# Key loads of an attention kernel: one DMA with a repeated source, or two DMAs of 64 rows

## The chip, the cores and the metric

The kernel runs on one core of one Trainium2 chip. The metric is the device time of one execution in microseconds, as the median of several runs. All durations in the rows below come from one execution that the hardware profiler recorded.

## What is computed

A two-layer encoder trunk for one prompt of 1024 positions and for 8 short groups of 16 positions with caches (1152 rows in all, width 1024). Layer 0 has sliding-window attention with 16 query heads over 4 key heads, a window of whole 64-row chunks, a sink for each head and a relative-position bias. Layer 1 has banded attention with 16 heads, each with its own keys and values, which are projected once from the output of layer 0. Each layer ends with an output projection, a normalisation and a gated feed-forward block with a short causal convolution. Cut to the attention:

```python
s = jnp.einsum('bqkgd,bskd->bkgqs', qg, k) * ATTN_SCALE + bias
s = jnp.where(valid, s, NEG_INF)          # own chunk and the 2 (layer 0) or 8 (layer 1) before it
p = softmax(s)                            # layer 0: with one more term, the sink
o = jnp.einsum('bkgqs,bskd->bqkgd', p, v)
```

## The kernel before, in words

Every float32 operand of a large product is held as two parts, a rounded high part and the rest as a low part, and a product is made of several matmuls of such parts.

The kernel projects queries, keys and values by matmul (mmT, L266, and mmX, L278). The keys of a layer are projected in `kproj` (L287): ScalarE (ACT) copies the high part out of PSUM (L297), VectorE (DVE) computes the low part (L298), and SyncE (SP) stores both to the DRAM tensor `kH` (L299), one row for each of the head's 64 dimensions and one column for each of 1024 positions. Values go the same way to `vH` in `vproj` (L326 to L328).

`attention` (L338) runs over 8 pairs `c` of heads and two heads `a` in each, and over 4 groups of 256 queries for each head, so 64 work items a layer. For one head it holds in SBUF the high keys `khi[a]`, the low keys `klo[a]` (128 partitions by 1024 columns) and the values `vst[a]`. The 64 key rows stand twice in a key tile, in partitions 0 to 63 and 64 to 127, because the query tile has the high part of the query in one half of the partitions and the low part in the other: one matmul with 128 rows (L504 with `khi`, L507 with `klo`) then makes two of the products. `kload` (L429) fills these tiles; `klo[1]` lies in the tile `wl`, the other three key tiles in `x1att`, and so the rows name them. A load of the next pair's head is issued from `finish` (L692), when the last scores and values of the present head with the same `a` are in the program: layer 1 does this for each head (L698), layer 0, where a key head serves four query heads, once for each `a` (L700).

After the scores come the softmax (DVE L470, ACT L474), the transposes of the probabilities (PE L530, split by ACT L535 and DVE L536), the products with the values (PE L549) and the store of the result from the Pool queue (L564). Between the heads, the 16 `items` of the small groups are worked off: their cached keys and values are loaded by SP (L597, L598, L603, L605), the value product is PE L650. Also between them, the query weights of the next pair (L164) and, towards the end of layer 1, the first weights of the output projection (`ws<-in_wo`, L164) are loaded; ACT rounds them (L149) and Pool or DVE takes the difference (L160).

All loads and stores but the bias loads, the attention output and the normalised rows are issued by SP, in one order, on one hardware queue (q1). Each engine works through its own instructions in order. That order comes from a scheduling pass that works with modelled durations when the kernel is built (L1340), not from the program's text alone.

Of the kernel before, what the change touches and what calls it, by code (L numbers as in the profile page):

```python
# [10 lines left out]
F32 = mybir.dt.float32  # L11
# [76 lines left out]
class Trunk:  # L88
# [249 lines left out]
    def attention(self, l, wk):  # L338
        nc, I = self.nc, self.I
# [76 lines left out]
        for p in range(2):  # L416
            t = sb.next()[:, 0:KS]
# [11 lines left out]
        def kload(c, a):  # L429
            row = c * 128 + 64 * a  # L430
            kh, kl = kH[0, row : row + 64, :], kH[1, row : row + 64, :]
            for t, k in ((khi[a], kh), (klo[a], kl)):
                nc.sync.dma_start(t.bitcast(F32), bass.AP(k.tensor, k.offset, [[0, 2], [1024, 64], [1, 1024]]))
            nc.sync.dma_start(
                vst[a].bitcast(F32), vH[:, 2 * c + a, :].rearrange("(k p) d -> p k d", p=128)
            )
# [255 lines left out]
        def finish(i):  # L692
            x = work[i]
            values(x)
            if x.g == 3:
                c, a = x.head.c, x.head.a
                if l == 1 and c < 7:
                    kload(c + 1, a)  # L698
                elif l == 0 and c == 3:
                    kload(1, a)  # L700
            if i == 6 * 8 - 1:
                sums(0)

        for a in range(2):
            kload(0, a)
# [638 lines left out]
```

## Time and profile before

| what | us |
|---|---|
| median of 3 runs | 3324.27 |
| lowest and highest run | 3322.79, 3326.6 |
| the profiled execution | 3324.77 |
| its span, from the first to the last instruction | 3322.8 |

The profile page gives, for each engine, the busy time and a strip of 40 slices of the span; each digit is the busy share of a slice of 83 us in tenths. PEclk is the granted clock of TensorE in tenths of full speed. The DMA strip is the mean busy share of 16 DMA engines. Attention of layer 0 is at about 85 to 440 us, the key and value projections of layer 1 at about 1580 to 1794 us, its attention at about 1794 to 2291 us. The feed-forward blocks fill most of the rest.

### The profile page before, as it was taken

The page shows a single profiled execution, that of the slowest core. Times are in us where ns is not written, and L with a number is a line of the kernel's source. Part 1 is how long each engine was busy: PE and PEld are TensorE (multiplying, and loading weights), DVE is VectorE, ACT ScalarE, POOL GpSimd, SP SyncE. Part 2 cuts the span into 40 slices and gives each one's busy share as a digit, 9 for nine tenths or more (in the row PEclk, how much of TensorE's full clock was granted, in tenths as well). Part 3 has the DMA queues.
Part 4 walks back from the last instruction along what each step waited for, and adds up shares of the span by engine and source line. Part 5 has one row for each costly group of instructions (what it writes and reads, how often), then busy time and mean ns, then how long its engine had stood idle before and what let it go on. Part 6 is the DMA issues. An engine that isn't in the chain of part 4 may idle for free. (4 is left out here: it accounts for less than half of the span.)

```text
span 3322.8 us, 42663 instructions
## 1 busy us (share of the span) xinstructions
PE 2927.7 (88%) x16524; PEld 2598.2 (78%) x16524; DVE 1553.0 (47%) x3162; ACT 1130.4 (34%) x2400; POOL 920.5 (28%) x745
## 2 busy tenths in 40 slices
PE   7697967899999999998898687656789999999996
PEld 5685755788888888887898676545679999999995
DVE  4253656524444444477014454335583444444457
ACT  3263622432222222226226454333244222222224
POOL 3021212423222222354531111110253222222253
PEclk8898988999999999999999897878899999999998
DMA  7343485622222222225664334347731111111121
GB/s 285 122 132 131 140 182 128 203 102 80 86 82 85 87 80 92 67 65 202 220 222 136 104 113 133 122 124 196 154 125 45 45 39 45 44 43 38 39 75 73
DMA packets 216282, 372.78 MB, mean 112 GB/s; under 512 B 34168, under 2 KB 138424, under 8 KB 215696
## 3 DMA queue, kind: packets, MB, share of 16 engines
q1 hardware_dynamic: 205808, 336.49, 32.6%
q0 software_dynamic: 10272, 33.56, 2.9%
q8 instruction: 130, 2.13, 0.3%
q14 instruction: 72, 0.59, 0.1%
HBM read 294.65 MB, written 84.79 MB: 114 GB/s over the span
## 5 line engine op out<-in xcount | busy, mean ns | idle before, releaser
L266 PE MATMUL PS<-H,wh 128*128 128x384 f32 (+1 forms) x5472 | 1060.7, 341 | 0.3 <-DVE H L160 0.3
L266 PEld LDWEIGHTS PS<-H,wh 128*128 128x128 f32 x5472 | 976.8, 190 | 17.1 <-issue 7.3
L266 PE MATMUL PS<-H,wl 128*128 128x384 f32 (+1 forms) x2736 | 575.5, 348 | 55.4 <-DVE X L327 22.7
L160 POOL TENSOR_TENSOR wl<-ws,wh 128x1024 fp32r<-128x1024 f32 x167 | 405.8, 2436 | 744.0 <-ACT wh L149 732.3
L981 DVE SCALAR_TENSOR_TENSOR F<-PS,F 128x256 f32<-128x256 f32 (+2 forms) x704 | 352.5, 512 | 491.7 <-ACT F L978 480.4
L266 PEld LDWEIGHTS PS<-H,wl 128*128 128x128 f32 x2736 | 495.0, 193 | 97.3 <-issue 43.8
L1052 PE MATMUL PS<-wh,X 128*128 128x512 f32 x1584 | 470.7, 396 | 18.4 <-DVE X L160 9.0
L978 ACT ACTIVATE F<-PS,F 128x384 f32<-128x384 f32 x264 | 177.2, 672 | 727.7 <-PE PS L266 724.7
L1052 PEld LDWEIGHTS PS<-wh,X 128*128 128x128 f32 x1584 | 294.9, 189 | 82.1 <-DVE X L160 11.0
L1043 DVE TENSOR_TENSOR acc<-acc,PS 128x512 f32<-128x512 f32 x324 | 221.4, 686 | 274.8 <-PE PS L1052 273.9
L1027 POOL TENSOR_TENSOR F<-F 128x384 f32<-128x384 f32 x132 | 138.9, 1053 | 649.3 <-ACT F L1025 643.8
L1052 PE MATMUL PS<-wl,X 128*128 128x512 f32 x792 | 247.1, 393 | 0.0
L149 ACT CAST wh<-ws 128x1024 fp32r<-128x1024 f32 x176 | 181.7, 1043 | 151.7 <-PE PS L1052 75.0
L278 PE MATMUL PS<-wh,H 128*128 128x256 f32 (+1 forms) x1008 | 199.4, 327 | 33.4 <-DVE H L160 24.9
L160 DVE TENSOR_TENSOR X<-F,X 128x384 fp32r<-128x384 f32 x132 | 151.6, 1149 | 99.6 <-ACT X L149 97.2
L278 PEld LDWEIGHTS PS<-wh,H 128*128 128x128 f32 x1008 | 154.3, 198 | 49.0 <-DVE H L160 26.1
L1052 PEld LDWEIGHTS PS<-wl,X 128*128 128x128 f32 x792 | 149.4, 189 | 33.6
L564 POOL DMA_DIRECT2D oT<-F x96 | 52.3, 545 | 441.3 <-ACT F L561 324.3
L530 PE MATMUL PS<-C,F 128*128 128x128 f32 x720 | 127.4, 294 | 38.1 <-DVE X L536 21.8
L470 DVE CUSTOM_DVE_ANT_0 F<-PS,F,C 128x256 f32<-128x256 f32 (+3 forms) x208 | 96.8, 480 | 93.9 <-PE PS L507 61.6
L470 DVE CUSTOM_DVE_ANT_0 F<-PS,F 128x320 f32<-128x320 f32 (+5 forms) x144 | 67.5, 480 | 142.8 <-issue 64.3
L530 PEld LDWEIGHTS PS<-C,F 128*128 128x128 f32 x720 | 90.5, 150 | 54.5 <-DVE X L536 24.0
(200 smaller groups left out, 3304.8 us busy)
## 6 DMA issues: line engine op xcount, KB each, us to landing
ws<-in_wup_dram SPq DMA_DIRECT2D x88, 512.0 KB
F<-in_adaw_dram SPq DMA_DIRECT2D x74, 512.0 KB
ws<-in_wdn_dram SPq DMA_DIRECT2D x44, 512.0 KB
ws<-in_adaw_dram SPq DMA_DIRECT2D x32, 512.0 KB
X<-oT SPq DMA_DIRECT2D x64, 256.0 KB
x1att<-kH SPq DMA_DIRECT2D x30, 512.0 KB
F<-xd SPq DMA_DIRECT2D x27, 512.0 KB
vH<-X SPq DMA_DIRECT2D x40, 256.0 KB
```

What stands on the lines that cost most here:

```text
L149: nc.scalar.copy(out, in_)
L160: self.eng(el).tensor_sub(lo, src, hi.bitcast(F32))
L266: self.nc.tensor.matmul(out[:, 0:n], w[a][:, k * 128 : k * 128 + 128], H[:, p, k, s0 : s0 + n], start=i == 0, stop=i == 23)
L278: self.nc.tensor.matmul(out[:, 0:n], H[:, p, j * kn + k, t0 : t0 + 128], w[a][:, k * n : k * n + n], start=i == 0, stop=i == 23,)
L470: nc.vector.tensor_tensor_reduce(out=p[:, c0 : c0 + w], in0=ps, in1=b, scale=1.0, scalar=init, op0=ALU.add, op1=ALU.min, accum_out=nm)
L530: nc.tensor.transpose(t[:, m * 128 : m * 128 + 128], p[:, (kt - k0) * 128 : (kt - k0) * 128 + 128], self.ident)
L564: nc.gpsimd.dma_start(self.oT[c, a, :, g0 : g0 + og * 256], x.head.o)
L978: nc.scalar.activation(y, ps[:, off : off + 384], AF.Identity, bias=w(3), scale=w(2))
L981: nc.vector.scalar_tensor_tensor(o, u, w(i), o, op0=ALU.mult, op1=ALU.add)
L1027: nc.gpsimd.tensor_mul(a, y, ya[bi])
L1043: nc.vector.tensor_add(row[:, n], row[:, n], ps)
L1052: nc.tensor.matmul(ps, ac[m][p][:, cs], w[m][q][:, n], start=i == 0, stop=i == 5)
```

## The change

`kload` issued one DMA for each key tile, whose source names the 64 rows twice through a leading dimension of 2 with step 0. It now issues two DMAs for each key tile, each from the plain 64 rows to one half of the partitions. The value load stays as it is. `kload` is called 20 times (4 times in layer 0, 16 times in layer 1), so 40 key DMAs of 512 KB become 80 of 256 KB.

```diff
             for t, k in ((khi[a], kh), (klo[a], kl)):
-                nc.sync.dma_start(t.bitcast(F32), bass.AP(k.tensor, k.offset, [[0, 2], [1024, 64], [1, 1024]]))
+                for b in range(2):
+                    nc.sync.dma_start(t[64 * b : 64 * b + 64, :].bitcast(F32), k)
```

## Rows read from the trace of the kernel before

**Rows 1.** The profile page: busy time by engine, strips of 40 slices
```profile
PE 2927.7 (88%) x16524; PEld 2598.2 (78%) x16524; DVE 1553.0 (47%) x3162; ACT 1130.4 (34%) x2400; POOL 920.5 (28%) x745
PE   7697967899999999998898687656789999999996
```

**Rows 2.** Waits of PE, 1780 to 2300 us: waiter, releaser, total us, times, longest
```profile
PE PS L507 <- DMA x1att<-kH: 51.2, 6, 13.1
PE PS L650 <- DMA F<-in_cvB_dram: 32.8, 4, 21.6
PE PS L530 <- DVE X L536: 21.8, 1, 21.8
PE PS L530 <- DVE wh L536: 14.5, 1, 14.5
PE PS L504 <- DVE x1att L457: 11.5, 1, 11.5
PE PS L507 <- DMA wl<-kH: 10.2, 1, 10.2
PE PS L504 <- DMA x1att<-kH: 3.1, 2, 2.2
```

**Rows 3.** Timeline of PE elsewhere: start, length, instruction, [idle before it, releaser]
```profile
123.32 2.90 PE L266 MATMUL PS<-H,wl 128*128 128x384 f32 x8 [22.65 <-DVE X L327]
264.42 0.48 PE L507 MATMUL PS<-x1att 128*128 128x128 f32 x1 [8.75 <-DMA x1att<-kH]
292.18 0.48 PE L507 MATMUL PS<-wl,x1att 128*128 128x128 f32 x1 [9.06 <-DMA wl<-kH]
1632.06 2.93 PE L266 MATMUL PS<-H,wl 128*128 128x384 f32 x8 [11.89 <-ACT F L305]
```

**Rows 4.** Windows: us; busy of PE, PEld, DVE, ACT, POOL; PEclk; DMA share; GB/s
```profile
88.00:93.00 5.00, 5.00 (x44) 5.00 (x43) 0.00 (x0) 0.00 (x0) 0.00 (x0) 1.00 0.13 52
...
1603.00:1608.00 5.00, 5.00 (x31) 5.00 (x30) 0.56 (x1) 0.48 (x1) 0.24 (x1) 1.00 0.13 52
...
2033.00:2038.00 5.00, 0.00 (x0) 0.00 (x0) 0.00 (x0) 0.00 (x0) 0.00 (x0) 0.50 0.13 52
```

**Rows 5.** Timeline of SP: start, length of the issue, line, transfer
```profile
1593.31 10.54 SPq L433 DMA_DIRECT2D x1att<-kH  x3
1603.89 9.93 SPq L299 DMA_DIRECT2D kH<-X  x1
...
1830.20 10.47 SPq L434 DMA_DIRECT2D x1att<-vH  x1
1840.71 10.62 SPq L433 DMA_DIRECT2D wl<-kH  x1
```

**Rows 6.** The chain that ended last, 1817 to 1850 us: start, us, what
```profile
1817.50 27.36 DMA x1att<-kH
1844.86 0.04 issue
```

**Rows 7.** Waits of ACT and DVE, 1780 to 2300 us
```profile
ACT x1att L149 <- DMA ws<-in_wo_dram: 39.5, 3, 21.0
DVE F L884 <- DMA F<-hmD: 11.9, 1, 11.9
```

**Rows 8.** Waits of ACT, whole span
```profile
ACT X L297 <- DMA kH<-X: 48.9, 9, 26.4
ACT X L326 <- DMA vH<-X: 37.8, 4, 23.1
```

**Rows 9.** Windows: after a stall, the whole attention of layer 1, and its ends
```profile
1845.00:1850.00 5.00, 5.00 (x16) 4.81 (x17) 2.02 (x5) 0.60 (x2) 0.00 (x0) 0.50 0.15 55
1872.00:1877.00 5.00, 5.00 (x35) 4.96 (x34) 1.93 (x7) 1.53 (x5) 0.84 (x3) 1.00 0.20 81
...
1795.00:1797.00 2.00, 2.00 (x8) 2.00 (x8) 1.94 (x4) 1.45 (x2) 0.00 (x0) 0.50 0.72 220
2289.00:2291.00 2.00, 0.99 (x7) 0.79 (x8) 2.00 (x3) 0.86 (x3) 0.55 (x1) 1.00 0.22 71
1795.00:2291.00 496.00, 351.98 (x2537) 312.14 (x2537) 225.51 (x707) 225.16 (x569) 69.30 (x115) 0.82 0.39 120
```

**Rows 10.** A window of the output projection, where SP issues 64-partition loads (L921)
```profile
2303.00:2306.00 3.00, 3.00 (x15) 2.43 (x14) 0.87 (x2) 0.22 (x1) 0.00 (x0) 1.00 1.22 229
```

**Rows 11.** Key load line: issue ns shortest, median, longest; first and last start
```profile
L433 SPq DMA_DIRECT2D x1att<-kH x30: 484/525/10615, 82.9 to 2213.1; - x30
```

**Rows 12.** The chain near the end: one weight load of 512 KB
```profile
3208.23 3.17 DMA ws<-in_wdn_dram
```

**Rows 13.** Timeline of SP, end of layer 1's attention: cached values of two items
```profile
2247.76 0.37 SPq L603 DMA_DIRECT2D F<-in_cvB_dram  x1
...
2258.07 0.37 SPq L603 DMA_DIRECT2D F<-in_cvB_dram  x1
```

## The prediction

> **What bounds the kernel now.** I first read the page: PE is busy for 88% of the span, and its strip shows where it is not [rows 1]. The weak stretch that touches this change is the run of sixes and fives around slices 22 to 27, the attention of layer 1. Next I asked who PE waits for in that stretch [rows 2]. The longest sum is a wait of the score matmuls for key tiles: 51.2 us on `x1att<-kH`, 10.2 us on `wl<-kH` and 3.1 us more at L504, 64.5 us in all. The window of the whole stretch [rows 9] has PE busy for 352 of 496 us, so 144 us idle, and nearly half of that names a key load directly. Two more such waits stand in layer 0, 8.75 and 9.06 us [rows 3].
>
> Then I asked why a key load is late. The chain shows one that took 27.36 us from issue to landing [rows 6], where a weight load of the same 512 KB took 3.17 us [rows 12]. The windows tell why: in three places where key loads alone were under way, the DMA share is 0.13 and the rate 52 GB/s [rows 4]. A share of 0.13 of 16 engines is two engines (2/16 = 0.125), and 524,288 bytes at 52 GB/s take 10.1 us. SP's timeline has the same number a third time: once some loads are queued, SP sits 10.47 and 10.62 us in a single issue, and it does so too for a value load and for a key store that merely come after key loads [rows 5]. So a key load runs on two of 16 engines for 10.1 us, and whatever SP has queued behind it, which needs those two engines as well, waits for it.
>
> That explains waits that do not name a key load. ACT waits for a weight of the output projection, 39.5 us in three waits [rows 7]; ACT works in order, so its PSUM copies of probabilities stop, and PE's transposes wait 21.8 and 14.5 us for an engine that itself has nothing to do [rows 2]. PE waits 32.8 us for cached values, `in_cvB` [rows 2]. DVE waits 11.9 us for `hmD` [rows 7] and hands that on to PE as 11.5 us at the first scores of layer 1 [rows 2]. ACT waits up to 23.1 us for a value store and 26.4 us for a key store to free a buffer [rows 8], which PE sees as 22.65 us at 123 us and as 11.89 us at 1632 us [rows 3].
>
> **The change, part by part.** *The transfer.* Two DMAs of 64 rows take the place of one whose source begins with a dimension of 2. The trace of before has no key load in the new form. Its nearest row is the window in which SP issues loads into 64 partitions [rows 10]: the DMA share is over 1 there (packet times overlap), so such loads use all 16 engines, not two. Bounds for a 512 KB tile: at the long end it stays at 10.1 us plus one more issue; at the short end it takes 1.3 us (two engines moved 52 GB/s, so 16 would move 416). I take the weight load's 3.17 us to landing [rows 12], since it is the nearest in size and in runs of 4 KB.
>
> The trace says 0.13 and 52 GB/s for the present form [rows 4]. [...]
>
> *SP's issue time.* 40 more issues, median 0.525 us each [rows 11], are 21 us of SP. They lie beside SP's blocked time: single issues of over 10 us [rows 5] go away, so I count nothing. If SP were the bound they would cost these 21 us.
>
> *The direct waits.* A load was issued at 1817.50 and PE began to wait 13.1 us before 1844.9, at 1831.8, so PE has 14.3 us of other work after the issue [rows 2, 6]. The new load of both tiles needs four issues, 2.1 us, and some 3.2 us to landing, 5.3 us together. It fits, so these waits go: 64.5 + 8.75 + 9.06 = 82.3 us.
>
> *The waits behind it.* 32.8 (cached values), 21.8 + 14.5 (weights through ACT), 11.5 (`hmD`), 22.65 (value stores) and 11.89 (key stores) sum to 115.1 us. Each has a transfer of its own that remains, so I give back about 2 us for each of some nine waits, 18 us.
>
> *The clock.* [...] The product of busy time and missing clock over all 248 windows of 2 us from 1795 to 2291 us (the first and the last are shown) sums to 37.6 us [rows 9]. Less stall means less of this; I keep back a quarter, 9 us.
>
> *What is late next.* Between stalls PE is busy 5.00 of 5.00 us at full clock [rows 9]: it is the bound as soon as the keys are there. DVE and ACT each have 225 us of work in the 496 [rows 9], which is 72% of the 314 us (352 - 37.6) that PE needs at full clock. Their queues drain today while PE stalls, and that rest goes away. The items keep one tile for cached values, and the next load can start only when the last one was used: even late in the stretch two such loads stand 10.3 us apart [rows 13], while two work items of PE will take about 2 x 314/64 = 9.8 us. The cost of both lies between 0 and some 40 us; I take 20 us.
>
> *Sum.* 82.3 + 115.1 + 37.6 = 235 us of losses that hang on the two busy engines; 18 + 9 + 20 = 47 us given back; gain 188 us. The profiled execution took 3324.77 us (3322.8 us of span and 2 us around it), half a microsecond over the median of the runs, so no correction is needed: 3324.8 - 188 = 3137 us.
>
> **The rivals.** (A) Forecast: 16 engines, the queue clears, PE becomes the bound. 3137 us; its own range is 3090 (nothing given back) to 3180 (twice the 47 us and no more).
>
> (B) The key waits go, but half of the rest comes back under other names, because ACT and DVE at 72% or the chain of the items hold PE. 82.3 + 0.5 x (115.1 + 37.6) = 159 us, less 47, is 112: 3213 us. For it: the order of each engine's work comes from modelled durations and will not fit the new transfers; every wait of PE passes through an in-order ACT. Against: in the stretches between stalls PE has no gap at all.
>
> (C) Everything comes back, and smaller waits that I left out as well: 3080 to 3090 us.
>
> (D) The change doesn't do what it says: each half still runs on two engines. Then the two halves need 5.05 us each, 10.1 us as before, and time stays at 3325 us. If in addition the 40 more issues lie on the path, 21 us come on top: 3346 us, slower. It decides at one point, the number of engines that a 64-row load gets. Against it stands the share over 1 for 64-partition loads [rows 10].
>
> **How the numbers follow.** I give (A) 0.70, (B) 0.19, (C) 0.06, and (D) 0.05, of which 0.02 without the cost of the issues and 0.03 with it. The likeliest gives 3137 us. The range for 8 in 10 has to take in (A), part of (B) and the edge of (C): 3080, the low end of (C), to 3215, just past the value of (B). About 0.2% of the time, 7 us, is what a measurement of this kernel can tell from no change: faster by more than that 0.95, within it 0.02, slower 0.03.
>
> **What would show it right or wrong.** In the profile after: the key load line should have 80 issues, none near 10 us, and no window of busy transfers at a share of 0.13 and 52 GB/s in the attention. SP should hardly be blocked in an issue. The waits of PE on `x1att<-kH` and `wl<-kH` should be under some 10 us in sum, the two long waits at L530 and ACT's wait for `in_wo` should be small, and the wait of 22.65 us at 123 us should be a few us. The granted clock of layer 1's attention should be above 0.95 and its length about 340 to 360 us. It would be wrong if key loads still move at 52 GB/s (then D), or if they move fast and PE's waits turn up at L504, L530 or L650 behind DVE, ACT or `in_cvB` (then B).

## The result, and the profile after

| | us |
|---|---|
| before, median (4 runs) | 3325.43 |
| after, median (4 runs) | 3090.66 |
| after, lowest and highest | 3085.17, 3098.18 |
| span of the profiled execution after | 3088.3 |
| ratio after to before, with its 95% interval | 0.9295 [0.9274, 0.9317] |

The change takes 234.8 us off, 7.1% of the time. Lines of the kernel below the key loads have a number one higher than before (L504 is now L505, and so on); in the runs k2 to k8 and p2 to p16 further down it is two higher.

The page after, busy times and the strip of PE (40 slices of 77 us), answers to [rows 1]:

```profile
PE 2884.1 (93%) x16524; PEld 2566.4 (83%) x16524; DVE 1545.2 (50%) x3162; ACT 1130.1 (37%) x2400; POOL 919.6 (30%) x745
PE   7999868899999999998999999866899999999996
```

PE does the same 16524 matmuls in 43.6 us less busy time (2927.7 to 2884.1), since more of them run at a higher granted clock (0.966 on average over the span, against 0.935 before): the time lost to the low clock, counted further down for three stretches, falls by 39.7 us. The fives and sixes of the attention of layer 1 are nines. The dip that is left there is the output projection behind it.

The key loads and the key stores after: shortest, median and longest issue in ns, first and last start. It answers to [rows 11]:

```profile
L434 SPq DMA_DIRECT2D x1att<-kH x60: 444/584/1444, 82.2 to 1982.2; - x60
L299 SPq DMA_DIRECT2D kH<-X x30: 359/383/1207, 54.6 to 1612.4; - x30
L434 SPq DMA_DIRECT2D wl<-kH x20: 455/584/1204, 100.6 to 1985.1; - x20
```

There are 80 issues, as forecast, and the longest takes 1.4 us where it took 10.6 us. The issue of a key store, which once took 9.93 us behind key loads [rows 5], now never takes more than 1.2 us.

Two windows of after, with the columns of [rows 4]: the stretch in which the first key loads are under way, and the whole attention of layer 1, which answers to the last line of [rows 9]:

```profile
88.00:93.00 5.00, 5.00 (x44) 5.00 (x43) 0.51 (x2) 0.37 (x1) 0.00 (x0) 1.00 1.05 257
1701.00:2045.00 344.00, 327.88 (x2545) 293.40 (x2546) 225.98 (x709) 224.50 (x570) 69.57 (x115) 0.96 0.61 173
```

The same five microseconds that had a DMA share of 0.13 and 52 GB/s now have a share of 1.05 (above 1, so packet times overlap) and 257 GB/s. Key loads are no longer alone in them: SP issued two weight loads at 87.3 us, where before it came to the first of these only at 93.4 us. The attention of layer 1 is 344 us long, not 498; PE is idle for 16 us of it, not 144, and the mean clock is 0.96, not 0.82.

Waits of PE in that stretch (1690 to 2052 us; the first row is the start of the output projection), and then the two of ACT and DVE that answer to [rows 7]; those of PE answer to [rows 2]:

```profile
PE PS L278 <- DVE H L160: 6.4, 1, 6.4
PE PS L651 <- DMA F<-in_cvB_dram: 5.5, 2, 4.0
PE PS L531 <- DVE X L537: 4.2, 1, 4.2
PE PS L505 <- DVE x1att L458: 3.4, 1, 3.4
```

```profile
ACT x1att L149 <- DMA ws<-in_wo_dram: 6.1, 2, 3.5
DVE F L885 <- DMA F<-hmD: 3.5, 1, 3.5
```

No wait for a key tile is left. Of the waits that stood behind the key loads, three are still there by name, and short: cached values 5.5 us (32.8), the transposes 4.2 us (36.3), the first scores 3.4 us (11.5). The two behind value stores and key stores (22.65 and 11.89 us) are gone.

**Where the time went.** The span in stages, cut at the first score, the last value product, the first matmul of an output projection and the first down-projection (L1052 before, L1053 after), all from the timeline of PE:

| stage | before us | after us | difference |
|---|---|---|---|
| start to the first score of layer 0 | 137.5 | 111.3 | -26.2 |
| scores and values of layer 0 | 299.1 | 265.7 | -33.4 |
| from there to the last down-projection of layer 0 | 1101.2 | 1100.9 | -0.3 |
| from there to the first score of layer 1 | 255.9 | 222.9 | -33.0 |
| scores and values of layer 1 | 498.2 | 344.4 | -153.8 |
| from there to the first down-projection of layer 1 | 226.8 | 238.2 | +11.4 |
| from there to the end | 804.1 | 804.8 | +0.6 |

The two spans differ by 234.5 us. All of it lies in the four stages in which key loads are issued or still under way; one stage behind them gives 11.4 us back.

### The profile page after: what moved, and what is told of

It reads as the page before. It is cut to its first block, busy times and chain, and to the rows that moved or that the text cites. A ratio compares the mean times of both kernels' runs of the same rounds, so it can differ in the third digit from the quotient of the medians.

```text
span 3088.3 us, 42738 instructions
## 1 busy us (share of the span) xinstructions
PE 2884.1 (93%) x16524; PEld 2566.4 (83%) x16524; DVE 1545.2 (50%) x3162; ACT 1130.1 (37%) x2400; POOL 919.6 (30%) x745
## 3 DMA queue, kind: packets, MB, share of 16 engines
q1 hardware_dynamic: 207008, 336.50, 36.2%
## 4 chain that ended last, share of the span: by engine, by line
PE 66%; DVE 7%; DMA 7%; POOL 3%; issue 3%; ACT 2%; SPq 1%; POOLq 0%; DVEq 0%; ACTq 0%
PE PS L266 40%; PE PS L1053 15%; PE PS L278 3%; PE PS L210 2%; PE PS L550 2%; PE PS L531 1%; POOL wl L160 1%; DMA ws<-in_wup_dram 1%; PE PS L505 1%; DMA X<-oT 1%; PE PS L508 1%; DMA F<-in_xrow_dram 1%; DVE F L943 1%; DMA x1att<-rD 1%; DMA F<-xd 1%
## 5 line engine op out<-in xcount | busy, mean ns | idle before, releaser
L266 PE MATMUL PS<-H,wl 128*128 128x384 f32 (+1 forms) x2736 | 567.3, 344 | 16.9 <-DVE H L151 7.8
L266 PEld LDWEIGHTS PS<-H,wl 128*128 128x128 f32 x2736 | 487.2, 190 | 59.0 <-issue 21.4
L1053 PE MATMUL PS<-wh,X 128*128 128x512 f32 x1584 | 470.8, 396 | 18.6 <-DVE X L160 9.4
L1053 PEld LDWEIGHTS PS<-wh,X 128*128 128x128 f32 x1584 | 294.9, 189 | 81.9 <-DVE X L160 11.0
L1053 PE MATMUL PS<-wl,X 128*128 128x512 f32 x792 | 247.4, 393 | 0.0
L1053 PEld LDWEIGHTS PS<-wl,X 128*128 128x128 f32 x792 | 149.9, 189 | 34.0
L1026 ACT ACTIVATE F<-F 128x384 f32<-128x384 f32 x132 | 69.2, 524 | 133.9 <-DVE F L982 129.3
L278 PE MATMUL PS<-x1att,H 128*128 128x512 f32 x432 | 115.9, 419 | 0.0
```

The source lines that it names most:

```text
L266: self.nc.tensor.matmul(out[:, 0:n], w[a][:, k * 128 : k * 128 + 128], H[:, p, k, s0 : s0 + n], start=i == 0, stop=i == 23)
L278: self.nc.tensor.matmul(out[:, 0:n], H[:, p, j * kn + k, t0 : t0 + 128], w[a][:, k * n : k * n + n], start=i == 0, stop=i == 23,)
L1026: nc.scalar.activation(y, y, AF.Gelu_apprx_tanh)
L1053: nc.tensor.matmul(ps, ac[m][p][:, cs], w[m][q][:, n], start=i == 0, stop=i == 5)
```

## Experiments

Two questions were open. Is it the number of engines that counts, or did the repeated source, the size of a DMA or another order of work do it? And do the parts add up?

The scheduling pass does lay out layer 1 in another order when the DMAs are cut in two (layer 0 keeps its order), so the order had to be held fixed while the transfer was slowed.

**k2, k4, k8: a small outermost dimension, first try.** The edit, with e = 2, 4 and 8 (here 2), on the changed kernel:

```diff
-                for b in range(2):
-                    nc.sync.dma_start(t[64 * b : 64 * b + 64, :].bitcast(F32), k)
+                s = bass.AP(k.tensor, k.offset, [[1024 * 32, 2], [1024, 32], [1, 1024]])
+                for b in range(2):
+                    nc.sync.dma_start(t[64 * b : 64 * b + 64, :].bitcast(F32), s)
```

> Two DMAs of 64 rows as in the changed kernel, same bytes, same count, and the same order of work on PE and ACT; only the source's rows are named as 2 groups of 32, so that its outermost dimension is 2 again, without a repeat. Theory 1 (the outermost dimension sets the number of engines): two engines, 5.05 us for a half tile, key loads at 52 GB/s and a DMA share of 0.13, time back at 3325 us, 3310 to 3350 with 40 more issues. Rival 2 (naming a row twice, or one DMA of 512 KB, is what was slow) and rival 3 (the new order of layer 1 brings the gain): 3091 us.

> As the run before, with 4 groups of 16 rows. Theory 1: four engines, 104 GB/s, 2.5 us for a half tile, 10.1 us for the four DMAs of high and low keys of one head. That is under the 14.3 us that PE has between an issue and its need, so the direct waits of PE on key loads (64.5 us in layer 1) are nearly gone, while transfers behind them are still held for up to 10 us: about 3150 us (3120 to 3200). Rivals 2 and 3: 3091 us.

> As the run before, with 8 groups of 8 rows. Theory 1: eight engines, 208 GB/s, 5 us for the four DMAs of one head: nearly all waits gone, 3100 us (3090 to 3125). Rivals 2 and 3: 3091 us.

Measured: 3082.26, 3086.57 and 3085.96 us, ratios 0.9291 [0.9272, 0.9309], 0.9303 [0.9288, 0.9319] and 0.9302 [0.9288, 0.9316]. Taken at face value that is what rivals 2 and 3 said. But in the built program the groups of consecutive rows were joined into one dimension of 64 again, so the DMAs were those of the changed kernel; the count of packets below, 207008 in all four, says the same. So these three runs decide nothing. They serve as repeats of the changed kernel: the four lie between 3082 and 3091 us, and closer by their ratios (0.9291 to 0.9303), since the kernel before, measured beside them, also took 6 us less than beside the first (3319.23 against 3325.43).

**p2, p4, p8, p16: a small outermost dimension that can't be joined.** The same edit with the rows named in strides, e = 2, 4, 8 and 16 (here 2):

```diff
+                s = bass.AP(k.tensor, k.offset, [[1024, 2], [1024 * 2, 32], [1, 1024]])
```

> Two DMAs of 64 rows as in the changed kernel, with the same bytes, the same count and the same order of work on PE, ACT and SP. The rows are named in another order, even rows first, so that the source's outermost dimension is 2 and can't be joined with the next one (in the runs k2, k4 and k8 the two were joined again when the kernel was built: their DMAs were those of the changed kernel). The keys' rows so stand in a wrong order and the scores are not the reference's. Theory 1 (the outermost dimension sets the number of engines): two engines, 52 GB/s, a DMA share of 0.13, 5.05 us for a half tile; time back at 3325 us, 3310 to 3370 with 40 more issues and an order of work that is laid out for other transfers. Rival 2 (naming a row twice, or one DMA of 512 KB, was slow) and rival 3 (the new order of layer 1 brings the gain): 3085 us.

> As p2 with 4 as the outermost dimension (every fourth row first). Theory 1: four engines, 104 GB/s, 2.5 us for a half tile, 10.1 us for the four DMAs of one head. That is under the 14.3 us that PE has between an issue and its need, so PE's direct waits on key loads (64.5 us in layer 1) are nearly gone, while transfers behind them are still held for up to 10 us: about 3150 us (3110 to 3200). Rivals 2 and 3: 3085 us.

> As p2 with 8 as the outermost dimension. Theory 1: eight engines, 208 GB/s, 5 us for the four DMAs of one head: nearly all waits gone, 3095 us (3085 to 3120). Rivals 2 and 3: 3085 us.

> As p2 with 16 as the outermost dimension (every sixteenth row first), so the source still has three dimensions and its rows a wrong order. If only the number of engines counts: the time of the changed kernel, 3082 to 3091 us. If the permuted naming of the rows costs something of its own, so that p2, p4 and p8 were slow in part for that: above 3100 us.

One window with key loads under way, in p2, p4 and p8 in turn (columns as in [rows 4]). In p2 they are alone in it; in p4 and p8 bias loads from the Pool queue move 24% and 40% of the bytes, so share and rate are those of both together:

```profile
1830.00:1834.00 4.00, 0.00 (x0) 0.00 (x0) 0.00 (x0) 0.00 (x0) 0.00 (x0) 0.50 0.13 51
```

```profile
1762.00:1766.00 4.00, 4.00 (x31) 3.96 (x31) 3.56 (x12) 2.78 (x8) 0.94 (x4) 1.00 0.25 103
```

```profile
1878.00:1880.00 2.00, 2.00 (x17) 1.85 (x15) 1.50 (x5) 1.68 (x5) 0.00 (x0) 1.00 0.50 201
```

The share is 2/16, 4/16 and 8/16, and the rate doubles each time: 25 to 26 GB/s for each engine. A window of p4 with key loads alone (1842 to 1845 us) has the same share, 0.25, and 102 GB/s.

The packets on SP's queue (q1 on each page) count the engines a second way. The packets of data are the same in all these runs; only packets of 4 bytes differ in number, and their differences fit one such packet for each engine of each key DMA: 40 x 2 before, 80 x 2, 4, 8 and 16 in p2, p4, p8 and p16, and 80 x 16 in the changed kernel and in k2, k4 and k8.

A third sign is what became of other transfers. In layer 1 SP issues weight loads of the output projection (`ws<-in_wo`, 512 KB) right behind key loads. Two of them stand on the chain that ended last in each of these runs. The two of before, with start and time from issue to landing:

```profile
2131.42 23.97 DMA ws<-in_wo_dram
2176.95 24.66 DMA ws<-in_wo_dram
```

The times follow:

| run | outermost dimension | DMA share | packets on q1 | us | ratio to before, 95% interval | waits of PE for key tiles, us | the two `in_wo` loads, us |
|---|---|---|---|---|---|---|---|
| before | 2 | 0.13 | 205808 | 3319.88 | | 82.4 | 24.0, 24.7 |
| p2 | 2 | 0.13 | 205888 | 3332.15 | 1.0038 [1.0025, 1.0051] | 92.4 | 21.0, 24.6 |
| p4 | 4 | 0.25 | 206048 | 3162.96 | 0.9530 [0.9514, 0.9546] | 11.2 | 16.4, 15.2 |
| p8 | 8 | 0.50 | 206368 | 3114.65 | 0.9386 [0.9371, 0.9401] | 0.4 | 10.2, 10.1 |
| p16 | 16 | not read alone | 207008 | 3080.19 | 0.9282 [0.9267, 0.9298] | 0 | 7.6, 5.7 |
| after2 (the changed kernel) | 64 | not read alone | 207008 | 3082.88 | 0.9292 [0.9272, 0.9312] | 0 | 6.4, 6.7 |

The time of before is the one measured beside p2, p4 and p8; beside p16 and after2 it was 3319.25 us. The last column but one sums the rows of PE's waits on `x1att<-kH` and `wl<-kH` over the whole span. Those of p2 and p4, with the waits that stand beside them:

```profile
PE PS L509 <- DMA x1att<-kH: 59.4, 7, 11.3
PE PS L652 <- DMA F<-in_cvB_dram: 35.7, 4, 23.0
PE PS L509 <- DMA wl<-kH: 25.8, 4, 10.4
PE PS L506 <- DMA x1att<-kH: 7.2, 4, 3.2
```

```profile
PE PS L652 <- DMA F<-in_cvB_dram: 14.9, 2, 14.2
PE PS L532 <- DVE X L538: 12.6, 2, 12.3
PE PS L532 <- DVE wh L538: 9.6, 2, 9.4
PE PS L509 <- DMA wl<-kH: 6.1, 2, 5.5
PE PS L509 <- DMA x1att<-kH: 5.1, 2, 4.0
```

What follows: with the bytes, the number of DMAs and the order of PE, ACT and SP all as in the changed kernel, two engines alone bring the old time back, and a little more: 12.3 us over the kernel before, measured beside it (3319.88). No row is named twice within a DMA there, and each DMA fills 64 partitions with 256 KB, as in the changed kernel, so neither the repeat nor the size was the cause (rival 2), nor is the new order (rival 3). The agreement of p16 with the changed kernel (3080.19 against 3082.88 us, measured beside each other) shows that naming rows in strides cost nothing of its own here.

p4 tells the two kinds of loss apart. PE's waits for key tiles have fallen from 92.4 to 11.2 us, since the four DMAs of a head now take 10.1 us by their rate; but transfers behind them are still held (the `in_wo` loads land after 15 to 16 us), and cached values (14.9 us) and the transposes behind ACT (22.2 us) cost more than the keys. p8 has 0.4 us of key waits left and is still 34 us slower than p16. By the stages of the two profiles 29 us of difference lie where key loads are issued or under way, 15 of them in the attention of layer 1, where PE is idle for 27 us in p8 and for 16 in p16; what lies in stages without key loads is not explained. So in p8 a head's key transfer still cost time, with PE's waits for keys down to 0.4 us. By the same arithmetic as in the prediction the four DMAs take 20.2, 10.1 and 5.0 us in p2, p4 and p8: each microsecond of that cost 17 us of the whole from 2 to 4 engines (169 us for 10.1) and 10 us from 4 to 8 (48 for 5.0), over 20 such loads. For 16 engines the arithmetic would give 2.5 us, but no run shows the 416 GB/s that this needs of key loads, so the last 34 us are not put to a length.

**l0only, l1only: the change in one layer.**

```diff
-                for b in range(2):
-                    nc.sync.dma_start(t[64 * b : 64 * b + 64, :].bitcast(F32), k)
+                if l == 0:
+                    for b in range(2):
+                        nc.sync.dma_start(t[64 * b : 64 * b + 64, :].bitcast(F32), k)
+                else:
+                    nc.sync.dma_start(t.bitcast(F32), bass.AP(k.tensor, k.offset, [[0, 2], [1024, 64], [1, 1024]]))
```

(l1only has `l == 1` there.)

> The new key loads in layer 0 only (4 of 20 calls); the order of work on PE and ACT is that of the kernel before. The trace after has layer 0 shorter by 26.2 us up to the first score and by 33.4 us from there to the last value product. If the loads alone do that: 3325 - 60 = 3266 us. If it needs the new order of work: 3325 us. The prediction's terms for layer 0 (22.65 + 8.75 + 9.06 = 40.5 us) would give 3285 us.

> The new key loads in layer 1 only (16 of 20 calls), with the changed kernel's order of work on PE and ACT. If the parts add up: layer 0 keeps its 60 us, so 3086 + 60 = 3146 us, within 10 us. If layers share a loss: less than that.

Measured: l0only 3263.96 us, ratio 0.9837 [0.9821, 0.9854]; l1only 3142.96 us, ratio 0.9466 [0.9450, 0.9482]. Against the kernel before, measured beside each (3319.23 and 3319.25), that is 55.3 and 176.3 us, 231.6 together, where the changed kernel, measured beside l1only, took 236.4 us off (3319.25 to 3082.88). The parts add up within 5 us. l0only has the order of work of the kernel before on PE and ACT, and yet layer 0 keeps the whole gain: its first score is at 111.3 us and its last value product at 376.7 us, as in the changed kernel. Four of the 20 calls of `kload` bring nearly a quarter of the gain.

**quarters, quarters2, after2: twice as many DMAs.**

```diff
-                for b in range(2):
-                    nc.sync.dma_start(t[64 * b : 64 * b + 64, :].bitcast(F32), k)
+                for b in range(4):
+                    nc.sync.dma_start(t[32 * b : 32 * b + 32, :].bitcast(F32), k[32 * (b % 2) : 32 * (b % 2) + 32, :])
```

> Four DMAs of 32 rows for each key tile, 160 in all, 80 more than the changed kernel. If SP's issue time is hidden, as the prediction counts it: 3087 us, within 10 us. If SP's issues lie on the path: 80 x 0.58 us = 46 us more, 3133 us.

> The run quarters again, beside the changed kernel on the same chip. If its 10 us less than the changed kernel are real and come from another order of work in the output projection of layer 1 (222.5 us from its first matmul to the first down-projection, against 231.8 us after and 227.7 us in p2, which has the changed kernel's order): a ratio to the changed kernel of 0.996 to 0.998. If they were chance: 1.000.

> The changed kernel again, for the run quarters2: 3082 to 3091 us.

Measured: quarters 3074.65 us, ratio 0.9267 [0.9253, 0.9281]; quarters2 3077.63 us, 0.9269 [0.9255, 0.9283]; after2, the changed kernel beside quarters2, 3082.88 us, 0.9292 [0.9272, 0.9312]. The key issues of quarters:

```profile
L434 SPq DMA_DIRECT2D x1att<-kH x120: 302/419/1776, 82.8 to 1981.5; - x120
L434 SPq DMA_DIRECT2D wl<-kH x40: 302/420/1408, 99.6 to 1983.5; - x40
```

160 issues of 0.42 us are 67 us of SP, 20 us more than 80 issues of 0.584 us, and they cost nothing; quarters even lies 2 us below the range expected of it. So SP's issue time is hidden, as the prediction counted it. Whether quarters is faster than the changed kernel is not settled: 5 us where the two ran beside each other, and the two intervals overlap. Its order of work differs in layer 1 (on PE from 1704 to 2222 us), so a small gain could come from there as well as from the loads.

**The 11 us given back.** From the first matmul of layer 1's output projection to the first down-projection, PE's timeline gives:

| order of work | runs | us |
|---|---|---|
| that of the kernel before | before, l0only | 221.2, 221.8 |
| that of the changed kernel | after, after2, k2, k4, k8 | 231.8, 227.3, 226.1, 228.5, 227.3 |
| that of the changed kernel | p2, p4, p8, p16, l1only | 227.7, 228.0, 228.5, 225.2, 225.1 |
| that of quarters | quarters, quarters2 | 222.6, 225.0 |

p2 has slow key loads and the changed kernel's order, and it is longer there as well. So some 4 to 7 us go with the order, not with the transfers; the rest of the 11 us is scatter, as after2 shows. These are single profiles, and the order of the kernel before has only two of them. Which instruction stands in the wrong place was not tried.

## Why the prediction was right, and where it was off

The forecast was 3137 us in a range of 3080 to 3215; measured were 3090.66 us. The direction and the mechanism hold: case (A), two engines against 16. The gain was 234.8 us, the forecast 188 us. The time lies at the very edge of the range that (A) was given for itself (3090 to 3180): the gain is as large as the whole sum of losses that the prediction listed, 235 us. That agreement is luck. About 37 us of it did come back, and as much was gained that the list did not have (see the sum below).

**The transfer.** Right. The share of 0.13 was read as two engines. That the outermost dimension sets the number was a theory until p2, p4 and p8 bore it out: for 2, 4 and 8 the share was 0.13, 0.25 and 0.50, and the rate 51, 103 and 201 GB/s. The 3.17 us to landing, taken from a weight load, were short: the one key load of the new form that stands on a chain, in k8, took 5.33 us, where the six of before on such chains took 23 to 29 us. Both 3.17 and 5.33 are well inside the 14.3 us of slack, so little hung on it.

**SP's issue time.** Counted at nothing, and quarters confirms it with twice as many issues. Rival (D)'s further 21 us have their counterpart in p2: 12.3 us over the kernel before, with two engines and 80 issues. What part of these the issues are was not separated.

**The direct waits.** Forecast to go, 82.3 us, and gone. The slack of 14.3 us, read from one load, was a fair size but not a floor: in p4, with 10.1 us of transfer, 11.2 us of waits are left.

**The waits behind it.** Right in kind: the transposes and the cached values fell with the key loads, in after and by steps in p2, p4 and p8, and so did the time to landing of the weight loads that ACT waits for. 18 us were kept back for nine waits. The three kinds that are left sum to 13.1 us (5.5, 4.2 and 3.4).

**The clock.** PE was busy at a granted clock of 0.50 from 1845 to 1850 us, behind a stall, and at 1.00 from 1872 to 1877, with none ahead of it [rows 9]. That less stall brings less of this was an estimate. The product of busy time and missing clock, in windows of 2 us as before, is 12.8 us in the attention of layer 1 after, with 16 us of idle PE in place of 144, where 9 were kept back of 37.6. Close. The mean clock of 0.96 and the length of 344 us are as the signs named (above 0.95, 340 to 360 us).

**What is late next.** This term was mis-sized: 20 us were kept back, and beside the waits counted above nothing of the kind is seen. DVE and ACT still have 226 and 225 us of work, now in 344 us, which is 66% of the stretch; PE's longest single wait between its first score and its last value is 4.2 us. The chain of the items, which I feared for, holds PE for 5.5 us in all.

**What the sum left out.** This is the larger error, 29 us. For layer 0 the terms were 22.65 + 8.75 + 9.06 = 40.5 us, and the two stages became 59.6 us shorter. For the projections of layer 1 they were 11.5 + 11.89 = 23.4 us, and the stage became 33.0 us shorter. Both held smaller waits and slow-clock work that I had seen only in the attention of layer 1: by the same count in windows of 2 us, work at a low clock lost 13.5 us in layer 0's attention before and 3.0 us after, and in the projections of layer 1 7.3 us before and 2.9 us after.

**The sum again.** 188 us forecast, plus 20 (late next), plus 19 and 10 (left out), plus 5 (behind: 13, not 18), less 4 (clock), less 11 (output projection) is 227; 8 us of the 234.8 remain without a name. Seen from the 235 us of listed losses: 13 (behind), 13 (clock) and 11 (output projection) came back, 37 us, and 19, 10 and 8 stood in no list, 37 us again.

**The rivals.** (B) would have shown waits at L504, L530 or L650 behind DVE, ACT or cached values; their counterparts after sum to 13.1 us. (C) is as near by its number (3080 to 3090). Its smaller waits were real, but that every loss is recovered does not hold, since 37 us came back. (D) fell with the first window at a share above 1; p2 is what it would have looked like.

## What to carry to other kernels

Read the DMA share of a window in which one kind of transfer is alone: here a share of 0.13, or 2/16, with a rate to match (52 GB/s) meant that this transfer ran on two engines, and the transfers behind it on the same queue were late as well (24 us for a weight load that takes 6 to 7 us after the change). Look for SP sitting ten microseconds in one issue (10.47 and 10.62 us here [rows 5]), and for engines that wait on each other in a chain while all are idle: here the cause was a load in the queue that none of them named. Two DMAs that each used all 16 engines, by their packets, beat one that used two (3090.66 against 3325.43 us), and 80 issues, or 160 (3074.65 and 3077.63 us), cost nothing here.

## What the runs showed of the hardware that was not expected

The rate of key loads followed the outermost dimension with hardly any loss: 51, 103 and 201 GB/s for 2, 4 and 8, with DMA shares of 0.13, 0.25 and 0.50 (at 4 and 8 with bias loads among them). For 2 it was the same whether a row was named twice (52 GB/s before) or not (51 GB/s in p2). A doubling from 8 to 16 is not shown: the window of after has 257 GB/s, among other loads.

The number of packets on SP's queue told the engines of the key DMAs: it grew by 80 for each further engine of the 80 key DMAs (205888, 206048, 206368 and 207008 for 2, 4, 8 and 16).

The two weight loads behind key loads on the same queue landed after 21 to 25 us when those ran on two engines, after 15 to 16, 10 and 6 to 8 us when they ran on 4, 8 and 16.

A key transfer that PE no longer waits for still cost time: from 8 to 16 engines, with 0.4 us of PE's waits on keys left, 34 us of the whole went away.

Groups of consecutive rows in a hand-written access pattern were joined when the kernel was built, so the outermost dimension written in k2, k4 and k8 was not the one their DMAs had (207008 packets, as in the changed kernel); only the strided form kept it (205888, 206048 and 206368 for 2, 4 and 8).
